# The delta rule's triangular inverse: four doublings on 32 by 32 diagonal blocks, held compactly

## The chip, the cores and the metric

The kernel runs on one core of a Trainium2 chip. The metric is the device time of one execution in microseconds (us). TensorE (PE) multiplies matrices, VectorE (DVE), ScalarE (ACT) and GpSimd (POOL) do elementwise work, SyncE (SP) issues transfers. Each engine works through its own list of instructions in order and waits at semaphores for the others.

## The reference, cut to what matters

The program is two layers of a network over 1024 positions of width 1024. The first layer mixes by a short convolution and sparse attention, the second by a gated delta rule with eight heads; each is followed by a gated feed-forward part and a gated embedding. The change lies in the delta rule of the second layer:

```python
kb = k * beta[..., None]
vb = v * beta[..., None]
m = jnp.where(strict, jnp.einsum('bhncd,bhnsd->bhncs', kb, k) * decay, 0.0)
t_inv = lax.linalg.triangular_solve(eye + m, jnp.broadcast_to(eye, m.shape), left_side=True, lower=True, unit_diagonal=True)
u = t_inv @ vb
w = t_inv @ (kb * jnp.exp(g)[..., None])

def step(state, xs):
    v_new = u_c - w_c @ state
    o = (q_c * jnp.exp(g_c)[..., None]) @ state + qk_c @ v_new
    state = state * jnp.exp(g_last)[..., None, None] + jnp.einsum('bhcd,bhce->bhde', k_dec, v_new)
```

For every head and chunk a unit triangular matrix is inverted; then a recurrence runs over the chunks of a head.

## The kernel before, in words

The delta rule is worked in chunks of 128 rows. A group is four chunks of one head, so eight heads of eight chunks make 16 groups. `l1_inv` (from line 1382) inverts the four matrices of a group side by side: `NM` holds minus the strict triangle, [128, 4, 128] in f32; `U` is to become the inverse (in transposed form) and `T` is its transpose.

The inverse grows by doublings. With the blocks of size n on the diagonal inverted, the off-diagonal block of size n in each pair follows from two products: `py` (NM times every second block of T's columns), copied out by ACT into `Y`, and `pz` (U times Y). DVE writes `pz` into the right places of `T` under a mask (`copy_predicated`, the masks are in `cm`), and a DVE transpose in 32 by 32 blocks gives `U` back. Lines 1460 to 1479 do this for n = 2, 4, 8 and 16 (k = 1 to 4) on full 128 by 128 matrices: four matmuls of 128x128 weights and 64 moving columns for `py`, four for `pz`. The first pairs (n = 1) come from POOL, lines 1457 and 1458: `NM` masked, plus the identity. The fifth doubling (lines 1482 to 1500, `py` with suffix 5) already works on 32 by 32 blocks, two or three positions of the array at once; the sixth (lines 1503 to 1514) on 64 by 64.

Each `yield` in `l1_inv` ends a step. `l1_mix` runs two groups' inverses alternately (two chains, ten steps apart), and between any two steps it lets a recurrence of an earlier group (`l1_rec`: `px`, `pn`, `pS`, `po`) take a step, and calls `F`, which issues some filling: matmuls of the projection (`l1_proj`, line 1340, 512 columns), after that of the output gate (`l1_z`, line 1589, 256 columns), near the end of the embedding (line 1022). How much filling stands between two steps follows from a count of steps and from fixed costs that each filling matmul yields, not from the steps' own length:

```python
us = max((L1_FILL - used[0]) / (2 * max(16 * L1_STEPS + L1_TAIL - done_steps, 1)), L1_MIN)
F(us)
rec()
F(us)
```

This is done under a manual schedule for TensorE, so TensorE executes the matmuls in just this order. The order of the other engines is chosen by a scheduler. `U` has three buffers, `T` and `Y` two.

Of the kernel before, what the change touches and what calls it, by code (L numbers as in the profile page):

```python
# [9 lines left out]
F32 = mybir.dt.float32  # L10
F32R = mybir.dt.float32r
BF16 = mybir.dt.bfloat16
I32 = mybir.dt.int32
U8 = mybir.dt.int8
AF = mybir.ActivationFunctionType
ALU = mybir.AluOpType
# [4 lines left out]
P = 128  # L21
# [14 lines left out]
QB0 = TOPK // P  # L36
NQB = NT - QB0

C_ID, C_CAUS, C_TRI, C_DM, C_UP0, C_ONE = 0, 128, 384, 512, 640, 768
NCF = 768  # L40


def _consts():
    r = np.arange(P)[:, None]
    c = np.arange(P)[None, :]
    f = np.zeros((P, NCF), np.float32)
    f[:, C_ID:C_ID + P] = r == c
    f[:, C_CAUS + P:C_CAUS + 2 * P] = np.where(c <= r, 0.0, NEG)
    f[:, C_TRI:C_TRI + P] = r <= c
    f[:, C_DM:C_DM + P] = np.where(c >= r, 0.0, NEG)  # L50
    f[:, C_UP0:C_UP0 + P] = (r // 2 == c // 2) & (r < c)
    m = np.zeros((P, 5, 64), np.int32)
    for k in range(1, 6):
        e = np.array([x for x in range(P) if not x >> k & 1])[None, :]
        m[:, k - 1] = ((((r ^ e) >> k) == 1) & (r > e))
    inv = lambda dim: (np.float32(1.0) / (np.float32(10000.0) ** (np.arange(0, dim, 2, dtype=np.float32) / np.float32(dim)))).astype(np.float32)
    fr = np.concatenate([inv(64), inv(32)])[None, :]
    return f, m, np.ascontiguousarray(fr)


class _K:
# [12 lines left out]
    def setup(self):  # L74
# [5 lines left out]
        self.dr = self.pool(self.es, "scr", space=DRAM)  # L80
        self.cf = self.const.tile([P, NCF], F32, name="cf")
        self.ident = self.cf[:, C_ID:C_ID + P]
# [1048 lines left out]
    def l1(self, close_h):  # L1131
        nc, A = self.nc, self.A
        self.oD = self.dr.tile([S, D], F32, name="oD")
        self.zD = self.dr.tile([S, D], F32, name="zD")
        self.cD = self.dr.tile([24, P, S], F32, name="cD")
        self.gD = self.dr.tile([2 * H, S], F32, name="gD")
        with self.phase("l1") as es:
            hp = self.pool(es, "l1hT")
            hT = self.hT_tiles((hp, hp), "1")
            sp = self.pool(es, "l1small")  # L1140
            self.cm = sp.tile([P, 5 * 64], I32, name="cm")
            nc.sync.dma_start(self.cm, A["cst_m"])
            da = self.pool(es, "l1a")
            cw = da.tile([P, 24, 4], F32, name="odcw")
            nc.sync.dma_start(cw, A["od_conv"])
            self.psum(es, "l1ps", tp0=1, tp1=1, st=2)
            self.ttags = itertools.cycle(["tp0", "tp1", "st", "st"])
            with ExitStack() as e2:
                nw = self.pool(e2, "l1norm")
                gB = self.bcast_row(self.np2, A["g_mix1"], D, "gB", "gB_mix1")  # L1150
                zab = self.l1_zab(nw, da, hT)
                for t in range(NT):
                    self.norm_T(self.np2, self.h[:, t, :], gB, hT, t, "n1", hnp=self.np)
                    if t:
                        next(zab)
                close_h()
                ab = [x for x in zab][-1]
                self.l1_gates(sp, nw, ab)
            db = self.pool(es, "l1b")
            self.goB = self.bcast_row(db, A["g_o"], P, "goB", "goB")  # L1160
            with self.tc.manual_schedule(engines={mybir.EngineType.PE}):
                self.l1_mix(da, db, hT, cw)
# [217 lines left out]
    def l1_inv(self, dp, hd, g, X, tag):  # L1380

        nc = self.nc
        v, gp = nc.vector, nc.gpsimd
        CH = lambda t: slice(t * P, (t + 1) * P)
        flat = lambda x: x.rearrange("p a b -> p (a b)")
        t0, nm = 4 * g, f"{hd}_{g}"
        X["step"] = 0
        G2 = lambda tg, bufs=2: dp.tile([P, 4, P], F32, tag=tg, bufs=bufs, name=f"{tg}{nm}")
# [52 lines left out]
        NM, AQ = G2("NM"), G2("AQ", 3)  # L1441
        X["step"] += 1
        yield True
        p = self.tp(f"pkk{nm}", tag)
# [6 lines left out]
        p = self.tp(f"pkq{nm}", tag)  # L1451
# [1 line left out]
            nc.tensor.matmul(p[:, CH(j)], kTn[:, j, :], cq[:, CH(j)], start=True, stop=True)  # L1453
        v.tensor_tensor(flat(AQ), p, flat(Dt), op=ALU.mult)

        U, T = G2("U", 3), G2("T")
        gp.tensor_tensor(U, NM, self.cf[:, None, C_UP0:C_UP0 + P].to_broadcast([P, 4, P]), op=ALU.mult)
        gp.tensor_tensor(U, U, self.ident[:, None, :].to_broadcast([P, 4, P]), op=ALU.add)
        v.transpose(flat(T), flat(U))
        for k in range(1, 5):  # L1460
            n = 2 ** k
            ev = lambda x: x.rearrange("p (b two n) -> p b two n", two=2, n=n)[:, :, 0, :]
            X["step"] += 1
            yield True
            py = self.tp(f"py{nm}_{k}", tag)
            for j in range(4):
                nc.tensor.matmul(py[:, j * 64:(j + 1) * 64], NM[:, j, :], ev(T[:, j, :]), start=True, stop=True)
            Y = G2("Y")
            nc.scalar.copy(flat(Y)[:, :256], py[:, :256])
            X["step"] += 1  # L1470
            yield True
            pz = self.tp(f"pz{nm}_{k}", tag)
            for j in range(4):
                nc.tensor.matmul(pz[:, j * 64:(j + 1) * 64], U[:, j, :], flat(Y)[:, j * 64:(j + 1) * 64], start=True, stop=True)
            sh = [P, 4, 64 // n, n]
            v.copy_predicated(T.rearrange("p a (b two n) -> p a b two n", two=2, n=n)[:, :, :, 0, :],
                              self.cm[:, (k - 1) * 64:k * 64].rearrange("p (b n) -> p b n", n=n)[:, None].to_broadcast(sh),
                              pz[:, :256].rearrange("p (a b n) -> p a b n", a=4, n=n))
            v.transpose(flat(U), flat(T))
        X["step"] += 1  # L1480
        yield True
        py = self.tp(f"py{nm}_5", tag)
        q = [slice(32 * x, 32 * x + 32) for x in range(4)]
        for j in range(4):
            for e, o in ((0, 1), (2, 3)):
                nc.tensor.matmul(py[q[o], q[j]], NM[q[e], j, q[o]], T[q[e], j, q[e]], start=True, stop=True)
        Y = G2("Y")
        for o in (1, 3):
            nc.scalar.copy(Y[q[o], 0, :], py[q[o], :P])
        X["step"] += 1  # L1490
        yield True
        pz = self.tp(f"pz{nm}_5", tag)
        for j in range(4):
            for e, o in ((0, 1), (2, 3)):
                nc.tensor.matmul(pz[q[e], q[j]], Y[q[o], 0, q[j]], U[q[o], j, q[o]], start=True, stop=True)
            nc.tensor.matmul(pz[q[1], q[j]], U[q[1], j, q[1]], Y[q[1], 0, q[j]], start=True, stop=True)
        blk = lambda x: pz[q[x], :P].rearrange("p (a b) -> p a b", a=4)
        v.tensor_copy(T[q[1], :, q[0]], blk(1))
        for e, o in ((0, 1), (2, 3)):
# [3 lines left out]
        py = self.tp(f"py6{nm}", tag)  # L1503
        for j in range(4):
            nc.tensor.matmul(py[64:, j * 64:(j + 1) * 64], NM[:64, j, 64:], T[:64, j, :64], start=True, stop=True)
        Y = G2("Y")
# [4 lines left out]
        pz = self.tp(f"pz6{nm}", tag)  # L1511
# [157 lines left out]

def _layout(I):  # L1670
    f, m, fr = _consts()
    L = {"cst_f": f, "cst_m": m.reshape(P, -1), "cst_fr": fr}
    I = {k: np.asarray(a) for k, a in I.items()}
# [48 lines left out]
```

## Time and profile before

| | us |
|---|---|
| median of three runs | 3055.42 (3049.29 to 3058.53) |
| the profiled execution | 3053.1 |
| its span, first to last instruction | 3051.3 |
| TensorE busy in the span | 2934.6 (96%) |
| DVE, ACT, POOL busy | 1911.4 (63%), 1269.5 (42%), 981.1 (32%) |
| projection matmuls (line 1340), first and last start | 1499.8 and 1988.7 |
| gate matmuls (line 1589), first and last start | 1989.0 and 2125.9 |
| first and last `py` of the four doublings (line 1467) | 1568.7 and 2112.0 |

How to read the rows: a timeline row gives start, duration, engine, line, what is written and from what, the tile of the array and the shapes; "x8" joins eight equal instructions in a row. An f32 matmul of the program shows as two records. Matmuls are pipelined, so records overlap, and a step's share of TensorE is seen from starts, not from durations. A row of lines has count, busy time, mean duration of one, and the idle time of the engine ahead of it.

### The profile page before, as it was taken

To read this page: it belongs to the slowest core of one execution; us is meant where nothing else is said; L and a number is where in the kernel's file an instruction comes from. 1 tells how busy PE (TensorE), PEld (TensorE's weight loads), DVE (VectorE), ACT (ScalarE), POOL (GpSimd) and SP (SyncE) were. 2 spreads that over 40 slices of the span, in tenths; PEclk is the share of its full clock that TensorE was granted. 3 is DMA by queue.
4 is the path that set the end of the run, shared out by engine and by line. 5 is a ranking of instruction groups with operands and counts; after the bars stand their busy time and mean duration, and the time that the engine had idled before them with its cause. 6 is when DMAs were issued, how large, how long until landed. Compare 5 with 4: busy or idle time off the path is not lost. (4 is left out here: it accounts for less than half of the span.)

```text
span 3051.3 us, 41382 instructions
## 1 busy us (share of the span) xinstructions
PE 2934.6 (96%) x16139; PEld 2473.5 (81%) x16139; DVE 1911.4 (63%) x3274; ACT 1269.5 (42%) x2225; POOL 981.1 (32%) x755
## 2 busy tenths in 40 slices
PE   7999999999999999999999999999999999989999
PEld 7989877787888877778888888898677888877877
DVE  5799985555444458963567777764545444458861
ACT  3558725544333334342445554443223333334341
POOL 1341000124444446523122222221134444455342
PEclk9999998999999999999999999999999999999999
DMA  4113174201222226423242222222721222254422
GB/s 143 49 49 100 47 242 152 90 28 73 104 104 104 101 101 257 135 100 120 85 144 96 81 91 90 91 87 89 274 76 66 104 104 104 104 198 164 137 92 90
DMA packets 119796, 340.55 MB, mean 112 GB/s; under 512 B 11568, under 2 KB 34608, under 8 KB 101936
## 3 DMA queue, kind: packets, MB, share of 16 engines
q1 hardware_dynamic: 119600, 337.91, 31.7%
q8 instruction: 127, 2.08, 0.3%
q14 instruction: 69, 0.57, 0.1%
HBM read 240.81 MB, written 97.06 MB: 111 GB/s over the span
## 5 line engine op out<-in xcount | busy, mean ns | idle before, releaser
L992 PE MATMUL pda<-sl 128*128 128x512 f32 x1056 | 251.4, 397 | 17.6 <-ACT sl L981 7.3
L992 PEld LDWEIGHTS pda<-sl 128*128 128x128 f32 x1056 | 202.3, 192 | 63.4 <-ACT sl L981 8.1
L778 POOL TENSOR_TENSOR S<-wr_gu 128x512 f32<-128x512 f32 x44 | 67.6, 1536 | 398.8 <-DMA wr_gu<-in_w_gu_dram 349.9
L992 PE MATMUL pdb<-sl 128*128 128x512 f32 x792 | 185.4, 392 | 2.1 <-ACT sl L981 1.1
L106 DVE TENSOR_TENSOR w2l_gu<-S,w2h_gu 128x1024 fp32r<-128x1024 f32 x44 | 73.4, 1667 | 173.9 <-ACT w2h_gu L105 173.9
L992 PEld LDWEIGHTS pdb<-sl 128*128 128x128 f32 x792 | 149.4, 189 | 34.6 <-DVE sl L982 1.9
L1340 PE MATMUL pso<-hh,wl_od 128*128 128x512 f32 x384 | 161.4, 420 | 0.0
L1340 PE MATMUL pso<-hl,wh_od 128*128 128x512 f32 x384 | 161.3, 420 | 0.0
L1340 PE MATMUL pso<-hh,wh_od 128*128 128x512 f32 x384 | 161.0, 419 | 0.0
L982 DVE TENSOR_TENSOR sl<-sl 128x1536 fp32r<-128x1536 f32 (+1 forms) x56 | 110.9, 1989 | 37.1 <-ACT sl L981 37.1
L981 ACT CAST sl<-sl 128x1536 fp32r<-128x1536 f32 (+1 forms) x56 | 76.6, 1374 | 133.2 <-DMA sl<-gfD 133.2
L1358 DVE SCALAR_TENSOR_TENSOR c<-pso,odcw,c 128x509 f32<-128x509 f32 (+1 forms) x144 | 107.1, 744 | 19.4 <-ACT c L1355 17.5
L776 POOL TENSOR_TENSOR T_dn<-wr_dn 128x512 f32<-128x512 f32 x44 | 78.9, 1821 | 101.1 <-PE pgb L847 52.1
L224 PE MATMUL pskqv<-wh_kqv,hh 128*128 128x256 f32 x384 | 109.5, 286 | 0.3 <-ACT wh_kqv L105 0.3
L224 PE MATMUL pskqv<-wh_kqv,hl 128*128 128x256 f32 x384 | 108.7, 283 | 0.0
L224 PE MATMUL pskqv<-wl_kqv,hh 128*128 128x256 f32 x384 | 108.3, 283 | 0.0
L105 ACT CAST w2h_gu<-S 128x1024 fp32r<-128x1024 f32 x44 | 46.3, 1052 | 147.1 <-PE pga L847 147.1
L600 DVE TENSOR_SCALAR_CACHE_REDUCE tk_junk<-sc,tk_f 128x1024 int8<-128x1024 f32 (+5 forms) x111 | 102.6, 924 | 1.8
L1110 PE MATMUL psp<-wh_pg,hh_p 128*128 128x512 f32 x256 | 101.6, 397 | 0.0
L1110 PE MATMUL psp<-wl_pg,hh_p 128*128 128x512 f32 x256 | 100.6, 393 | 0.0
L1110 PE MATMUL psp<-wh_pg,hl_p 128*128 128x512 f32 x256 | 100.5, 393 | 0.0
L597 ACT ACTIVATE tk_junka<-sc,tk_f 128x512 int8<-128x512 f32 (+2 forms) x93 | 83.7, 900 | 36.8 <-DVE tk_f L615 30.5
(531 smaller groups left out, 9055.6 us busy)
## 6 DMA issues: line engine op xcount, KB each, us to landing
wr_gu<-in_w_gu_dram SPq DMA_DIRECT2D x44, 1024.0 KB
sl<-gfD SPq DMA_DIRECT2D x42, 768.0 KB
gfD<-Sg SPq DMA_DIRECT2D x22, 1024.0 KB
wr_dn<-in_w_dn_dram SPq DMA_DIRECT2D x22, 1024.0 KB
wr_od<-in_w_qkv_dram SPq DMA_DIRECT2D x12, 1024.0 KB
cD<-c SPq DMA_DIRECT2D x24, 512.0 KB
gfD<-g SPq DMA_DIRECT2D x22, 512.0 KB
wr_z<-in_w_z_dram SPq DMA_DIRECT2D x10, 1024.0 KB
```

The source lines that it names most:

```text
L106: self.nc.vector.tensor_tensor(lo, src, hi.bitcast(F32), op=ALU.subtract).ins)
L224: nc.tensor.matmul(out, a[:, kc, c], b[:, kc, :], start=(kc == 0 and i == 0), stop=(kc == KC - 1 and i == 2))
L597: nc.scalar.activation(jk[:, :n], sc[b], AF.Sign, bias=fb, scale=-1.0, accum_out=c)
L600: v.tensor_scalar(jk[:, :n], sc[b], fb, 0.0, op0=op, op1=ALU.add, accum_out=c)
L776: sub = lambda o, x, y: eng.tensor_tensor(o, x, y, op=ALU.subtract)
L778: eng.tensor_tensor(dst[0], b[2], b[3], op=ALU.add)
L981: nc.scalar.copy(y, x.bitcast(F32))
L982: v.tensor_tensor(x, x.bitcast(F32), y.bitcast(F32), op=ALU.subtract)
L992: nc.tensor.matmul(ps, a[:, i, c], b[:, i, :], start=first and i == 0 and k == 0, stop=i == m - 1 and k == 2, skip_group_check=True)
L1110: nc.tensor.matmul(ps, a[:, kc, c], b, start=kc == 0 and i == 0, stop=kc == KC - 1 and i == 2)
L1340: nc.tensor.matmul(ps[:, f * 512:(f + 1) * 512], a[:, kc, :], b[f][:, kc, :], start=(kc == 0 and i == 0), stop=(kc == KC - 1 and i == 2))
L1358: nc.vector.scalar_tensor_tensor(c[:, e:(f + 1) * 512], ps[:, e - d:(f + 1) * 512 - d], cw[:, k:k + 1], c[:, e:(f + 1) * 512], op0=ALU.mul ...
```

## The change

The first four doublings touch only the 32 by 32 blocks on the diagonal. The changed kernel holds these blocks compactly: `U32` and `T32` are [128, 4, 32] tiles in which the 32 rows of block b lie on partitions 32b to 32b+31. A `py` or `pz` step is now 16 matmuls (four chunks, four blocks), each with 32x32 weights and 16 moving columns, on the four diagonal positions of the array. The ACT copy, the predicated copy and the DVE transpose work on the compact tiles, a quarter as long. `U` and `T` are filled with zeros by POOL at the start, and after the fourth doubling POOL copies the blocks into them (four copies for `U`, two for `T`, which is only kept as its upper left 64 rows and columns). The first pairs are four POOL products on 32 partitions and one sum. The fifth doubling reads `U32` and `T32`. The masks shrink to four of 16 columns, and the constants change to suit.

```diff
-        U, T = G2("U", 3), G2("T")
-        gp.tensor_tensor(U, NM, self.cf[:, None, C_UP0:C_UP0 + P].to_broadcast([P, 4, P]), op=ALU.mult)
-        gp.tensor_tensor(U, U, self.ident[:, None, :].to_broadcast([P, 4, P]), op=ALU.add)
-        v.transpose(flat(T), flat(U))
+        q = B32
+        small = lambda tg, n=32: dp.tile([P, 4, n], F32, tag=tg, bufs=2, name=f"{tg}{nm}")
+        U, T = G2("U", 3), small("T", 64)
+        gp.memset(U, 0.0)
+        gp.memset(T[:64], 0.0)
+        U32, T32 = small("U32"), small("T32")
+        for b in q:
+            gp.tensor_tensor(U32[b], NM[b, :, b], self.cf[b, None, C_UP0:C_UP0 + 32].to_broadcast([32, 4, 32]), op=ALU.mult)
+        gp.tensor_tensor(U32, U32, self.cf[:, None, C_I32:C_I32 + 32].to_broadcast([P, 4, 32]), op=ALU.add)
+        v.transpose(flat(T32), flat(U32))
...
             for j in range(4):
-                nc.tensor.matmul(py[:, j * 64:(j + 1) * 64], NM[:, j, :], ev(T[:, j, :]), start=True, stop=True)
-            Y = G2("Y")
-            nc.scalar.copy(flat(Y)[:, :256], py[:, :256])
+                for b in q:
+                    nc.tensor.matmul(py[b, j * 16:(j + 1) * 16], NM[b, j, b], ev(T32[b, j, :]), start=True, stop=True)
+            Y = small("Yc", 16)
+            nc.scalar.copy(flat(Y), py[:, :64])
...
             for j in range(4):
-                nc.tensor.matmul(pz[:, j * 64:(j + 1) * 64], U[:, j, :], flat(Y)[:, j * 64:(j + 1) * 64], start=True, stop=True)
-            sh = [P, 4, 64 // n, n]
-            v.copy_predicated(T.rearrange("p a (b two n) -> p a b two n", two=2, n=n)[:, :, :, 0, :],
-                              self.cm[:, (k - 1) * 64:k * 64].rearrange("p (b n) -> p b n", n=n)[:, None].to_broadcast(sh),
-                              pz[:, :256].rearrange("p (a b n) -> p a b n", a=4, n=n))
-            v.transpose(flat(U), flat(T))
+                for b in q:
+                    nc.tensor.matmul(pz[b, j * 16:(j + 1) * 16], U32[b, j, :], Y[b, j, :], start=True, stop=True)
+            sh = [P, 4, 16 // n, n]
+            v.copy_predicated(T32.rearrange("p a (b two n) -> p a b two n", two=2, n=n)[:, :, :, 0, :],
+                              self.cm[:, (k - 1) * 16:k * 16].rearrange("p (b n) -> p b n", n=n)[:, None].to_broadcast(sh),
+                              pz[:, :64].rearrange("p (a b n) -> p a b n", a=4, n=n))
+            v.transpose(flat(U32), flat(T32))
+        for b in q:
+            gp.tensor_scalar(U[b, :, b], U32[b], 1.0, None, op0=ALU.mult)
+        for b in q[:2]:
+            gp.tensor_scalar(T[b, :, b], T32[b], 1.0, None, op0=ALU.mult)
...
-                nc.tensor.matmul(py[q[o], q[j]], NM[q[e], j, q[o]], T[q[e], j, q[e]], start=True, stop=True)
+                nc.tensor.matmul(py[q[o], q[j]], NM[q[e], j, q[o]], T32[q[e], j, :], start=True, stop=True)
...
-                nc.tensor.matmul(pz[q[e], q[j]], Y[q[o], 0, q[j]], U[q[o], j, q[o]], start=True, stop=True)
-            nc.tensor.matmul(pz[q[1], q[j]], U[q[1], j, q[1]], Y[q[1], 0, q[j]], start=True, stop=True)
+                nc.tensor.matmul(pz[q[e], q[j]], Y[q[o], 0, q[j]], U32[q[o], j, :], start=True, stop=True)
+            nc.tensor.matmul(pz[q[1], q[j]], U32[q[1], j, :], Y[q[1], 0, q[j]], start=True, stop=True)
```

TensorE, where a group's second chain ends its fourth doubling and the next group begins its first (names: `pso` is the filling, `pz_1_4` the fourth `pz` of one group, `py_0_1` the first `py` of the next). Before:

```order
L1340 MATMUL pso_13949<-hl_1_11707,wh_od_13176 128x512
L1340 MATMUL pso_13949<-hh_1_11706,wl_od_13177 128x512
L1474 MATMUL pz_1_4_14114<-Y_1_14078,U_1_13754 128x64 x4
L1340 MATMUL pso_13949<-hh_1_11706,wh_od_13176 128x512
L1340 MATMUL pso_13949<-hl_1_11707,wh_od_13176 128x512
L1340 MATMUL pso_13949<-hh_1_11706,wl_od_13177 128x512
L1340 MATMUL pso_13949<-hh_1_11706,wh_od_13176 128x512
L1467 MATMUL py_0_1_14143<-T_0_14095,NM_0_14022 128x64 x4
L1340 MATMUL pso_13949<-hl_1_11707,wh_od_13176 128x512
```

The same place in the changed kernel:

```order
L1343 MATMUL pso_14319<-hl_1_11707,wh_od_13340 128x512
L1343 MATMUL pso_14319<-hh_1_11706,wl_od_13341 128x512
L1485 MATMUL pz_1_4_14539<-Yc_1_14496,U_1_14085 32x16 x16
L1343 MATMUL pso_14319<-hh_1_11706,wh_od_13340 128x512
L1343 MATMUL pso_14319<-hl_1_11707,wh_od_13340 128x512
L1343 MATMUL pso_14319<-hh_1_11706,wl_od_13341 128x512
L1343 MATMUL pso_14319<-hh_1_11706,wh_od_13340 128x512
L1477 MATMUL py_0_1_14586<-T_0_14517,NM_0_14416 32x16 x16
L1343 MATMUL pso_14319<-hl_1_11707,wh_od_13340 128x512
```

Nothing has moved: each step of four matmuls has become one of sixteen small ones at the same place, with the same filling around it.

POOL, at the start of the same group's inverse (`kd` belongs to the group, `qe`, `dec` and `egl` to later ones; brackets name the semaphores waited for; `U32` and `T32` are printed as U and T). Before:

```order
L1439 TENSOR_TENSOR kd_0_14020<-kR_0_13856,dec_0_13837 128x512 [waits DVE_49,Activation_49]
L1457 TENSOR_TENSOR U_0_14094<-NM_0_14022,cf 128x512 [waits DVE_49]
L1458 TENSOR_TENSOR U_0_14094<-U_0_14094,cf 128x512 [waits Pool_49]
L1398 TENSOR_TENSOR qe_1_14276<-lq_1_13891,EGb_1_13897 128x512 [waits DMAHW4_49,DMAHW1_49,PE_49]
L1400 TENSOR_SCALAR egl_1_14278<-EGb_1_13897 128x4 [waits DVE_49]
```

In the changed kernel:

```order
L1442 TENSOR_TENSOR kd_0_14414<-kR_0_14214,dec_0_14195 128x512 [waits DVE_49,Activation_49]
L1466 TENSOR_TENSOR U_0_14516<-NM_0_14416,cf 32x128 [waits DVE_49]
L1466 TENSOR_TENSOR U_0_14516<-NM_0_14416,cf 32x128 [waits Pool_49]
L1466 TENSOR_TENSOR U_0_14516<-NM_0_14416,cf 32x128 x2
L1462 MEMSET U_1_15085 128x512 [waits PE_49,Pool_49]
L1467 TENSOR_TENSOR U_0_14516<-U_0_14516,cf 128x128
L1401 TENSOR_TENSOR qe_1_14779<-lq_1_14261,EGb_1_14267 128x512 [waits DMAHW4_49,DMAHW1_49,PE_49]
L1403 TENSOR_SCALAR egl_1_14781<-EGb_1_14267 128x4 [waits DVE_49]
L1494 TENSOR_SCALAR T_1_14082<-T_1_14086 32x4x32 [waits DVE_49]
L1494 TENSOR_SCALAR T_1_14082<-T_1_14086 32x4x32 [waits Pool_49]
```

Two operations have become five, the zeros for the next group's `U` stand between the products and the sum, and the copies into `T` come after `qe`. The memset's semaphore of PE is that of the last `pn` which reads the buffer's former `U`, in the recurrence three groups back; on TensorE that `pn` stands ahead of this group's `pkq` (line 1453), which stands ahead of the `pz_1_4` above.

## Rows read from the trace of the kernel before

**Rows 1.** Windows in the stage: us, busy us and instructions per engine, clock, DMA, GB/s.

```profile
core 0: us, PE busy (x) PEld busy (x) DVE busy (x) ACT busy (x) POOL busy (x), PEclk, DMA share, GB/s
1700.00:1850.00 150.00, 148.38 (x1124) 126.84 (x1123) 110.83 (x323) 76.39 (x177) 41.90 (x43) 1.00 0.27 92
1989.00:2126.00 137.00, 136.27 (x1325) 132.07 (x1324) 74.87 (x240) 49.42 (x128) 25.59 (x24) 1.00 0.22 76
```

**Rows 2.** Waits of TensorE, 1560 to 2126 us: total us, times, longest.

```profile
PE pS L1546 <- DVE vn L1542: 2.6, 4, 1.2
PE pz L1495 <- ACT Y L1489: 2.3, 2, 1.7
```

**Rows 3.** Lines, 1560 to 2126 us, TensorE: count, busy us, mean ns, idle before.

```profile
L1467 PE MATMUL py<-T,NM 128*128 128x64 f32 x512 | 64.8, 270 | 0.1
```

**Rows 4.** Line 1467 alone, 1988.9 to 2126 us: ns min/median/max, first and last start.

```profile
L1467 PE MATMUL py<-T,NM x120: 217/275/275, 1990.9 to 2112.0; 128*128 128x64 f32 x120
```

**Rows 5.** Timeline of TensorE between 512-column matmuls: start us, us, instruction.

```profile
1704.49 0.39 PE L1340 MATMUL pso<-hh,wh_od 128*128 128x512 f32 x1
1704.71 1.00 PE L1467 MATMUL py<-T,NM 128*128 128x64 f32 x8
...
1705.84 0.39 PE L1340 MATMUL pso<-hh,wl_od 128*128 128x512 f32 x1
...
1706.29 0.40 PE L1340 MATMUL pso<-hl,wh_od 128*128 128x512 f32 x1
1706.62 0.44 PE L1486 MATMUL py<-T,NM 32*32 32x32 f32 x16
...
1707.32 0.40 PE L1340 MATMUL pso<-hh,wh_od 128*128 128x512 f32 x1
...
1709.61 0.40 PE L1340 MATMUL pso<-hh,wh_od 128*128 128x512 f32 x1
1709.93 0.22 PE L1495 MATMUL pz<-U,Y 32*32 32x32 f32 x2
...
1710.19 0.19 PE L1496 MATMUL pz<-Y,U 32*32 32x32 f32 x1
...
1710.65 0.40 PE L1340 MATMUL pso<-hh,wl_od 128*128 128x512 f32 x1
```

**Rows 6.** Timeline of TensorE between 256-column matmuls.

```profile
2074.14 0.28 PE L1589 MATMUL psz<-wl_z,hh 128*128 128x256 f32 x1
2074.26 1.00 PE L1467 MATMUL py<-T,NM 128*128 128x64 f32 x8
...
2075.28 0.28 PE L1589 MATMUL psz<-wh_z,hh 128*128 128x256 f32 x1
...
2081.70 0.28 PE L1589 MATMUL psz<-wl_z,hh 128*128 128x256 f32 x1
2081.91 0.44 PE L1486 MATMUL py<-T,NM 32*32 32x32 f32 x16
...
2082.51 0.28 PE L1589 MATMUL psz<-wh_z,hh 128*128 128x256 f32 x1
```

**Rows 7.** Timeline at the start of one inverse; brackets: idle before, releaser.

```profile
1697.42 1.13 DVE L1448 SCALAR_TENSOR_TENSOR NM<-pkk,nbeta,Dt 128x128 f32<-128x128 f32 x4 [1.12 <-PE pkk L1446]
...
1698.62 1.28 POOL L1457 TENSOR_TENSOR U<-NM,cf 128x512 f32<-128x512 f32 x1 [9.97 <-DVE NM L1448]
...
1699.72 0.38 PE L1540 MATMUL pn<-x,U 128*128 128x128 f32 x2
...
1699.98 1.28 POOL L1458 TENSOR_TENSOR U<-U,cf 128x512 f32<-128x512 f32 x1
...
1701.29 0.71 DVE L1459 STREAM_TRANSPOSE T<-U 128x512 f32<-128x512 f32 x1 [0.80 <-POOL U L1458]
```

**Rows 8.** Lines, 1560 to 2126 us, small operations of DVE and POOL.

```profile
L1542 DVE TENSOR_SCALAR vn<-pn,beta 128x128 f32<-128x128 f32 x60 | 20.5, 342 | 19.4 <-PE pn L1540 19.1
...
L1392 POOL TENSOR_TENSOR dec<-Dt,G 128x4 f32<-128x4 f32 x14 | 2.9, 206 | 24.4 <-DMA Dt<-gD 21.0 <-DVE rsq_a L135 1.6 <-DVE rsq_y L137 1.4
```

More of the change, by code (lines that the diff above doesn't have):

```diff
@@ L37 @@
 NQB = NT - QB0
-C_ID, C_CAUS, C_TRI, C_DM, C_UP0, C_ONE = 0, 128, 384, 512, 640, 768
-NCF = 768
+C_ID, C_CAUS, C_TRI, C_DM, C_UP0, C_I32 = 0, 128, 384, 512, 640, 672
+NCF = 704
+B32 = [slice(32 * x, 32 * x + 32) for x in range(4)]
 def _consts():
@@ L50, in _consts @@
     f[:, C_DM:C_DM + P] = np.where(c >= r, 0.0, NEG)
[L51 to L54, printed above, removed]
+    r, c = r % 32, c[:, :32]
+    f[:, C_UP0:C_UP0 + 32] = (r // 2 == c // 2) & (r < c)
+    f[:, C_I32:C_I32 + 32] = r == c
+    m = np.zeros((P, 4, 16), np.int32)
+    for k in range(1, 5):
+        e = np.array([x for x in range(32) if not x >> k & 1])[None, :]
         m[:, k - 1] = ((((r ^ e) >> k) == 1) & (r > e))
@@ L1140, in l1 @@
             sp = self.pool(es, "l1small")
-            self.cm = sp.tile([P, 5 * 64], I32, name="cm")
+            self.cm = sp.tile([P, 4 * 16], I32, name="cm")
             nc.sync.dma_start(self.cm, A["cst_m"])
@@ L1482, in l1_inv @@
         py = self.tp(f"py{nm}_5", tag)
-        q = [slice(32 * x, 32 * x + 32) for x in range(4)]
         for j in range(4):
             for e, o in ((0, 1), (2, 3)):
-                nc.tensor.matmul(py[q[o], q[j]], NM[q[e], j, q[o]], T[q[e], j, q[e]], start=True, stop=True)
+                nc.tensor.matmul(py[q[o], q[j]], NM[q[e], j, q[o]], T32[q[e], j, :], start=True, stop=True)
         Y = G2("Y")
```

## Prediction

> **What bounds the kernel now.** I read the windows first, cut at the borders of the delta-net stage (the second mixer: `l1_mix`, from the first inverse step at about 1560 us to the last gate matmul at 2126 us). In 1700 to 1850 TensorE is busy 148.38 of 150 us and in 1989 to 2126 it is busy 136.27 of 137, while DVE, ACT and POOL have 110.83, 76.39 and 41.90 of 150 us in the first of these [rows 1]. The reader is to see that this stage ends when TensorE has worked through its list, and that the list never runs dry: the work of the inverse stands between matmuls of the projection (L1340) and later of the gate (L1589), which need nothing from it. The waits of TensorE in the stage come second: the two longest entries are 2.6 and 2.3 us in total, so almost nothing is lost to late operands [rows 2]. A gain must therefore be a shorter TensorE list, and a shorter latency alone would bring nothing.
>
> How long an instruction stands in that list is not its duration, since matmuls overlap. It is read from starts in the timeline: from the last filling matmul ahead of a step to the second one behind it, because the first one behind also starts late.
>
> **The step that is changed.** Per group of four 128-row chunks the four doublings take a `py` and a `pz` each; with 16 groups that is 128 steps. The lines show it: 512 records of `py`, eight a step (four f32 matmuls, each recorded twice), so 64 steps [rows 3]; `pz` has the same loop. 120 of these 512 fall after 1988.9 us, where the filling is the gate's 256 columns wide [rows 4]: 15 `py`, with as many `pz` 30 steps; the other 98 stand between 512-column matmuls.
>
> - Cost now. Between 512-column matmuls: 1704.49 to 1705.84, 1.35 us for a step and two fillings [rows 5]. Between 256-column ones: 2074.14 to 2075.28, 1.14 us [rows 6].
> - Cost then. A step becomes 16 matmuls (32 records) of 32x32 weights and 16 moving columns, four blocks on the diagonal, each with rows and columns of the array to itself. No row shows four such blocks at once, but the fifth doubling is the same thing with fewer: `py_5` has 16 records on two blocks and takes 1706.29 to 1707.32, 1.03 us; `pz_5` has 24 records on three blocks and takes 1709.61 to 1710.65, 1.04 us [rows 5]. Eight records more cost 0.01 us: the 24 starts lie between 1709.93 and 1710.19, 0.26 us, and the 16 of `py_5` take as long (0.44 less one record's 0.19). So the time goes by rounds (four chunks, two records each, eight rounds of about 0.031 us), and another block in a round is nearly free. I take 0.01 more for the fourth block, 1.05 us. Between 256-column matmuls `py_5` takes 2081.70 to 2082.51, 0.81 us [rows 6]; two more blocks make 0.83. Both spans hold the idle time ahead of small blocks, which these steps already pay.
> - Bounds. Below: if a round follows the moving columns, of which there are 16 instead of 32, half of the 0.25 us goes, 0.125 us a step or 16 us in all on top. Above: if the four blocks took a round each, 32 times 0.031 us is 1.00 instead of 0.25 us, the step 1.79 us, slower than now. I stay with 1.05, next to the nearest row.
> - Sum. 98 x (1.35 - 1.05) + 30 x (1.14 - 0.83) = 29.4 + 9.3 = 38.7 us off TensorE's list.
>
> Here a rule speaks against the change. In the rows above two row groups of `py_5` write into one `py` tile of 512 f32 a partition, and their starts don't line up behind each other. The Trainium skill (TensorEngine Tiling (Array Packing), Gotcha 1: PSUM Pressure) says that different row tiles cannot access the same PSUM bank at once. By it the four blocks, all in one tile, would go one after another and the sum would be that of the upper bound; the trace does not agree for two row groups, so I give it a small chance for four. A second page (TensorE: Matmul & The Clock Gate, the section "Wait — 56ns, not 53.3ns?") has a floor of about 25 ns from start to start: 32 of these are an estimated 0.8 us, which would also undo the gain; 24 starts in 0.26 us (11 ns each) don't agree with it for different blocks.
>
> **What else it moves.** TensorE's order in the stage stays as it was, step for step, so each step keeps the filling around it.
>
> - Evacuation and transposes shrink: 80 DVE transposes of 128x512 at 0.71 us become 128x128, 64 predicated copies go from 256 to 64 elements a partition, 64 ACT copies too. These engines aren't the bound, so I cost it at nothing; it shortens every latency between steps, by as much as the filling between them shortens.
> - The start of the inverse: POOL made `U` by two operations of 1.28 us after DVE's last `NM` (end 1698.55), DVE's transpose ended at 1702.00, and the first `py` began at 1704.71: 2.7 us in hand [rows 5, 7]. Now POOL does four small products, for every other group a memset of the next group's `U`, and one sum. Bounds for a small one (128 elements a partition): 0.206 us, the row with 4, and 1.28, the row with 512 [rows 7, 8]; by elements between them 0.47 us, which I take. The memset at most 1.28. With 0.08 us between operations (the gap of the two POOL rows) 5 x 0.47 + 1.28 + 6 x 0.08 = 4.1 us, then at most 0.71 for the transpose: 1703.4. The memset waits for a `pn` of the recurrence that began at 1699.72 and took 0.38 us here [rows 7], earlier than the products end (about 1700.8), so this wait is free; behind it stand the sum and, through the transpose, `py`. One shortened `pz` lies between, so `py` would start at 1704.4: 1 us still in hand.
> - The six copies back into `U` and `T`: two of `T` (1.1 us) are needed by the sixth doubling, behind `py_5` and `pz_5`, which alone stand 3.3 us apart (1706.62 and 1709.93) [rows 5]; `U`'s later still. Hidden. In all POOL loses 32 x 1.28 = 41 us and gets at most 16 x (11 x 0.47 + 1.28 + 0.64) = 114, the second memset taken at half the first. Its busy share of a quarter has the room.
>
> I add 1 us for new waits: 3053.1 (the profiled execution, 3051.3 of span and 1.8 around it) - 38.7 + 1 = 3015.4. The median shown is 2.3 above the profiled execution, so 3017.7, say 3018.
>
> **Rivals.**
>
> 1. The recurrence takes part of it back. Between `px`, `pn` and `pS` DVE must answer (`vn` has 60 instructions [rows 8], `x` about as many), and about half of these 120 answers have a shortened step beside them. If each lost the whole 0.30 us, 60 x 0.30 = 18 us come back: 3036. For it: the longest wait on the list is just this one, `pS` for `vn` [rows 2]. Against: 2.6 us over 60 is next to nothing, so most have slack, and DVE is relieved.
> 2. Only two blocks run at once. 16 rounds are 0.50 us, the step 1.30: 128 x 0.05 = 6 us off, 3049, no change that can be measured. For it: two blocks with both rows and columns of their own are all that a row shows (the third of `pz_5` shares its rows with another). Against: that third one was free though it shares. The same time comes out if every small POOL operation cost 1.28 us: the chain then takes 6 x 1.28 + 0.5 + 0.7 = 8.9 us after 1698.6 and ends 3.1 us after 1704.4; over 16 groups with the memset in half of them, some 40 us of waits cancel the gain. The 0.206 us row speaks against it.
> 3. Slower: the four blocks take a round each, because they share a PSUM tile or cannot start in so quick a sequence. Place: the 128 steps; price: 1.79 - 1.35 = 0.44 us each, 56 us, so 3111. It turns to a loss when 32 starts take more than 0.25 + 0.30 = 0.55 us, 17 ns a start. Against: 11 ns a start with three blocks [rows 5].
>
> **How the numbers follow.** Forecast 0.76 (3006 to 3026, by the bounds of the step's cost), first rival 0.10 (3026 to 3040), second 0.08, third 0.06. A difference below 0.3% (9 us) cannot be told from none: faster 0.86, same 0.08, slower 0.06. The range from 3006 to 3038 holds the forecast and most of the first rival.
>
> **What would show it.** In the profile after: the `py` and `pz` steps between 512-column matmuls at 1.0 to 1.1 us from the filling ahead to the second behind, with 32 starts inside 0.3 us; the stage from the first projection matmul to the last gate matmul shorter by 36 to 40 us; TensorE's waits in the stage still below 8 us, none of `py` on POOL's `U`; everything behind the stage as long as before. Wrong it is if four blocks stretch the starts, if `py` waits for the transpose at the beginning of a group, or if the granted clock, 1.00 in both windows [rows 1] (the 2.4 GHz level), falls in the stage because the steps hold more idle time in relation to work.

## The result, and the profile after

| | before | changed | |
|---|---|---|---|
| median of runs | 3052.36 us (4 runs, 3043.74 to 3058.53) | 3018.2 us (4 runs, 3012.98 to 3021.66) | ratio 0.9889, 95% interval 0.9859 to 0.9919 |
| measured again, another chip | 3054.2 us (7 runs) | 3012.37 us (4 runs, 3010.24 to 3017.35) | ratio 0.9868, 0.9849 to 0.9886 |
| profiled execution | 3053.1 us | 3017.34 us | -35.8 us |

The kernel became 34 to 42 us (1.1 to 1.3%) faster; 3018 had been forecast.

The first reading is of windows. Two of the changed kernel lie inside the two fillings, as those of [rows 1] did (same columns):

```profile
1700.00:1850.00 150.00, 147.22 (x2100) 112.01 (x2097) 106.14 (x340) 81.10 (x189) 59.33 (x90) 1.00 0.32 104
1960.00:2091.00 131.00, 128.39 (x2086) 118.53 (x2083) 67.33 (x240) 48.73 (x133) 44.99 (x69) 1.00 0.26 82
```

TensorE is still busy for 98% of both, so its list still sets the end of the stage. The bound has not moved to another engine; the list has become shorter. By how much is read from the first projection matmul to the last gate matmul. The two groups of matmuls by their lines, before (ns min/median/max, first and last start):

```profile
L1340 PE MATMUL pso<-hh,wh_od x384: 387/395/628, 1499.8 to 1987.4; 128*128 128x512 f32 x192
...
L1589 PE MATMUL psz<-wh_z,hl x192: 274/283/385, 1989.2 to 2125.9; 128*128 128x256 f32 x192
```

and after:

```profile
L1343 PE MATMUL pso<-hh,wh_od x384: 387/396/628, 1504.8 to 1960.8; 128*128 128x512 f32 x192
...
L1603 PE MATMUL psz<-wh_z,hl x192: 276/282/387, 1962.3 to 2091.0; 128*128 128x256 f32 x192
```

The window over this stretch, before:

```profile
1499.80:2126.00 626.20, 620.18 (x4741) 544.09 (x4740) 423.00 (x1228) 288.50 (x652) 140.10 (x142) 1.00 0.27 91
```

and after:

```profile
1504.70:2091.20 586.50, 577.70 (x7814) 467.66 (x7813) 378.96 (x1228) 278.58 (x652) 202.06 (x313) 1.00 0.30 98
```

The stage lasts 586.2 us (1504.8 to 2091.0) instead of 626.1, 39.9 less, though TensorE has 3073 records more in it. DVE has 44 us less to do there, ACT 10 us less, POOL 62 more. Behind the stage nothing changed: the program ends 924.6 us after the last gate matmul, 925.4 before. The stage began 5.0 us later than in the profile of before, which is why the span is only 35.7 us shorter.

Where the 39.9 us come from, the step shows. The timeline of TensorE between 512-column matmuls, to be laid beside the first rows of [rows 5]:

```profile
1699.25 0.40 PE L1343 MATMUL pso<-hh,wh_od 128*128 128x512 f32 x1
1699.58 0.44 PE L1477 MATMUL py<-T,NM 32*32 32x16 f32 x32
1699.95 0.50 PE L1343 MATMUL pso<-hl,wh_od 128*128 128x512 f32 x1
1700.29 0.39 PE L1343 MATMUL pso<-hh,wl_od 128*128 128x512 f32 x1
...
2042.89 0.28 PE L1603 MATMUL psz<-wl_z,hh 128*128 128x256 f32 x1
2043.10 0.44 PE L1477 MATMUL py<-T,NM 32*32 32x16 f32 x32
2043.47 0.38 PE L1603 MATMUL psz<-wh_z,hl 128*128 128x256 f32 x1
2043.69 0.28 PE L1603 MATMUL psz<-wh_z,hh 128*128 128x256 f32 x1
```

From the filling ahead to the second one behind it are 1.04 us, and 0.80 in the 256-column part, answering to [rows 6]. The first block matmul starts 0.33 us behind the filling; 32 of them start in 0.26 us (0.44 less one record's 0.18); 0.11 us later comes the filling, and 0.34 after it the next. Two fillings alone take 0.46 us (1698.79 to 1699.25 in the same timeline). So a step is 0.26 us of starts and 0.31 us that TensorE needs to go over to the small blocks and back. The medians over all steps between two such fillings without a wait are 1.032 and 0.802 us; measured in the same way before they are 1.355 and 1.131. The list became shorter by 98 x 0.323 + 30 x 0.329 = 41.5 us.

What came back are waits. TensorE's waits in the stage, 1560 to 2091 us (total us, times, longest), answering to [rows 2]:

```profile
PE tpk L1439 <- DVE kR L1415: 1.9, 2, 0.9
PE pz L1485 <- ACT Yc L1479: 1.6, 1, 1.6
PE pS L1560 <- DVE vn L1556: 1.5, 3, 1.0
PE py L1519 <- POOL o L1580: 1.0, 1, 1.0
```

With six smaller entries (2.3 us in all) they come to 8.3 us, against 5.9 before (two smaller entries included). The gaps of TensorE over the whole stage, the width of the two windows above less its busy time, are 8.8 us, against 6.0.

The last of these rows names POOL, but it is no wait for POOL's new copies. The `py` of the sixth doubling waits for DVE, ACT and POOL at once; POOL's copies into `T` had ended at 1959.16, and the `py` came right behind ACT's copy into `U`:

```profile
1965.97 0.51 ACT L1514 COPY U<-pz 32x128 f32<-32x128 f32 x2
...
1966.57 0.65 PE L1519 MATMUL py<-T,NM 64*64 64x64 f32 x8 [0.98 <-POOL o L1580]
```

The start of an inverse, answering to [rows 7] (brackets: idle before, releaser):

```profile
1692.84 1.13 DVE L1451 SCALAR_TENSOR_TENSOR NM<-pkk,nbeta,Dt 128x128 f32<-128x128 f32 x4 [1.45 <-PE pkk L1449]
...
1694.04 1.97 POOL L1466 TENSOR_TENSOR U<-NM,cf 32x128 f32<-32x128 f32 x4 [7.24 <-DVE NM L1451]
...
1696.08 0.53 POOL L1462 MEMSET U<- 128x512 f32 x1
1696.66 0.46 POOL L1467 TENSOR_TENSOR U<-U,cf 128x128 f32<-128x128 f32 x1
1697.20 0.30 DVE L1468 STREAM_TRANSPOSE T<-U 128x128 f32<-128x128 f32 x1
```

`T32` is there at 1697.50, 3.5 us after the last `NM`, just as long as before (1698.55 to 1702.00); the `py` that reads it starts at 1699.58, so 2.1 us are in hand.

### The profile page after: what moved, and what is told of

It reads as the page before. It is cut to its first block, busy times and chain, and to the rows that moved or that the text cites. A ratio compares the mean times of both kernels' runs of the same rounds, so it can differ in the third digit from the quotient of the medians.

```text
span 3015.6 us, 47722 instructions
## 1 busy us (share of the span) xinstructions
PE 2891.6 (96%) x19211; PEld 2396.3 (79%) x19211; DVE 1873.3 (62%) x3274; ACT 1259.5 (42%) x2225; POOL 1043.9 (35%) x931
```

## The experiments

All are edits of the changed kernel, timed against the kernel before on the same chip. "Stage" is the time from the first projection matmul to the last gate matmul, 586.2 and 585.0 us in two profiles of the changed kernel. Where the granted clock fell, "lost to the clock" is an estimate, the sum over windows of 2 us of width times (1 - clock): 1.7 and 0.0 us in these two profiles, 1.7 in that of before. The theory was that the gain is the shorter step on TensorE's list and nothing else; the rivals put it on shorter evacuations and transposes, or saw a cost on POOL that eats part of it.

**1. The long transposes back.** `U32` and `T32` lie in tiles four times as wide, so the transpose is 128x512 again; the matmuls stay.

```diff
-        U32, T32 = small("U32"), small("T32")
+        Uw, Tw = small("U32", 128), small("T32", 128)
+        gp.memset(Uw, 0.0)
+        gp.memset(Tw, 0.0)
+        U32, T32 = Uw[:, :, :32], Tw[:, :, :32]
...
-            v.transpose(flat(U32), flat(T32))
+            v.transpose(flat(Uw), flat(Tw))
```

> The changed kernel, but U32 and T32 lie in tiles four times as wide and DVE transposes all 128x512 again (80 transposes at about 0.71 us instead of 0.31, some 32 us more work for DVE, and 0.4 us more between a step and the one two steps on); POOL fills the wide tiles with zeros. TensorE's list is that of the changed kernel. My theory (the gain is TensorE's shorter list alone): as the changed kernel, within 3 us of 3018, steps still 1.03 us apart. Rival (part of the gain is the relief of DVE and the shorter latency): 10 to 20 us of the gain are lost, about 3030 to 3040, with TensorE's waits on DVE grown by as much.

Measured: 3015.8 us, ratio 0.9878 (0.9862 to 0.9893), stage 587.4. The line of the transpose in the changed kernel (count, busy us, mean ns, idle before):

```profile
L1490 DVE STREAM_TRANSPOSE U<-T 128x128 f32<-128x128 f32 x64 | 19.8, 309 | 0.8
```

and in this one:

```profile
L1493 DVE STREAM_TRANSPOSE U<-T 128x512 f32<-128x512 f32 x64 | 45.3, 708 | 0.8
```

Each step's answer from DVE takes 0.40 us longer and the time is that of the changed kernel. TensorE's gaps are 11.4 us, 2.3 to 2.6 more than in the two profiles of the changed kernel (8.8 and 9.1), so the shorter transposes are worth some 2 us at most. The copies of ACT and DVE stayed short here; the next experiment covers them.

**2. Block by block.** The same 16 matmuls in another order: all four chunks of one block, then the next block.

```diff
-            for j in range(4):
-                for b in q:
+            for b in q:
+                for j in range(4):
```

> The changed kernel with the two loops of a step exchanged: all four chunks of one block, then the next block, so that eight records in a row fall on the same position of the array. Same matmuls, same data. My theory (records of one position follow each other at 0.031 us, records of different positions run side by side): a step's 32 starts take about 32 x 0.031 = 1.0 us instead of 0.25, the step 1.78 us instead of 1.03, and the kernel 128 x 0.75 = 96 us longer than the changed one, about 3114, slower than before. Rival (starts are paced by something that counts records, such as the issue of instructions): no change, 3018. In between, if the queue can look past the records of one position: 0.3 to 0.6 us a step, 3030 to 3060.

Measured: 3068.8 us, ratio 1.0054 (1.0039 to 1.0069), stage 639.7. Slower than before, by the order of 16 matmuls. The step (TensorE, start and duration):

```profile
1701.48 0.40 PE L1343 MATMUL pso<-hh,wh_od 128*128 128x512 f32 x1
1701.81 0.88 PE L1477 MATMUL py<-T,NM 32*32 32x16 f32 x32
1702.62 0.50 PE L1343 MATMUL pso<-hl,wh_od 128*128 128x512 f32 x1
1702.95 0.39 PE L1343 MATMUL pso<-hh,wl_od 128*128 128x512 f32 x1
```

1.47 us instead of 1.04; 32 starts take 0.70 us instead of 0.26. The single records show why. Four records of each step last 198 ns, the others about 178; read as the first record of each block, these four start at 0, 153, 307 and 460 ns. From its first one a block's eight records follow each other after 52 ns and then after 31 to 32, so the next block begins when five of the eight have started. In the changed kernel's order the four long records start at 0, 7, 13 and 20 ns, and each block then goes on at the same distances. So the blocks run wholly beside each other only if they come in turn; block by block they overlap by less than half. Everything else of the change, the shorter copies and transposes too, is still in this kernel, and the whole gain is gone: the gain lies in the matmuls. By the medians of the step (1.472 and 1.242) the stage should be 98 x 0.117 + 30 x 0.111 = 14.8 us longer than before; it is 13.6 longer (with 5.1 us lost to the clock, 3.4 more than before). The expected 3114 was too high, since it left out the overlap at each change of block. The point at which the gain was to turn to a loss, 0.55 us for 32 starts, lies between the two measured values.

**3. Twice the moving columns.** Full 32 columns of `T32` and `Yc` instead of every second block.

```diff
-                    nc.tensor.matmul(py[b, j * 16:(j + 1) * 16], NM[b, j, b], ev(T32[b, j, :]), start=True, stop=True)
-            Y = small("Yc", 16)
+                    nc.tensor.matmul(py[b, j * 32:(j + 1) * 32], NM[b, j, b], T32[b, j, :], start=True, stop=True)
+            Y = small("Yc", 32)
```

> The changed kernel with all 32 moving columns in each block matmul instead of the 16 that are needed (ACT then copies 128 columns instead of 64, about 0.05 us more each). My theory (a round is set by the loading of the 32-column weights, not by the moving columns): starts still within 0.26 us, step 1.03, kernel within 3 us of 3018. Rival (a round follows the moving columns, or four blocks of 32 columns crowd the PSUM tile): the starts take 0.35 to 0.5 us and the kernel is 12 to 32 us longer, 3030 to 3050.

Measured: 3012.21 us, ratio 0.9868 (0.9852 to 0.9884), stage 588.7. The step's record:

```profile
1702.34 0.45 PE L1477 MATMUL py<-T,NM 32*32 32x32 f32 x32
```

Its starts take 0.45 less 0.19, 0.26 us, as with 16 columns. Here a round of four blocks does not follow the moving columns; the lower bound of the forecast (a round that follows them) is out. By the median the step is 1.045 us, 0.013 longer, and the kernel is 6 us below the forecast, no more than two measurements of the changed kernel differ (experiment 10).

**4. Every block matmul twice.**

```diff
-            for j in range(4):
+            for j in (0, 1, 2, 3, 0, 1, 2, 3):
```

> The changed kernel with every block matmul of the four doublings issued twice (64 records a step, same result). My theory (TensorE's list ends the stage, each round of four blocks costs 0.031 us): 0.25 us more a step, 128 x 0.25 = 32 us, 3050, about as long as before. Rival (the steps lie in time that TensorE would spend waiting anyway): under 10 us more, below 3028.

Measured: 3070.96 us, ratio 1.0057 (1.0035 to 1.0079), stage 639.5, 53 us longer than the changed kernel's. Two steps in TensorE's timeline, the second behind a wait (in brackets):

```profile
1700.52 0.73 PE L1477 MATMUL py<-T,NM 32*32 32x16 f32 x64
...
1927.36 1.03 PE L1485 MATMUL pz<-Yc,U 32*32 32x16 f32 x64 [2.75 <-ACT Yc L1479]
```

The list of TensorE's waits has these together (total us, times, longest):

```profile
PE pz L1485 <- ACT Yc L1479: 8.8, 6, 2.7
```

And the windows from the end of two of them on, the one of 2.75 us and one of 1.28 (columns as in [rows 1]):

```profile
1926.00:1942.00 16.00, 14.64 (x252) 10.33 (x252) 5.46 (x11) 6.42 (x15) 5.53 (x9) 0.57 0.14 52
2002.00:2018.00 16.00, 15.79 (x276) 14.16 (x277) 9.17 (x16) 5.10 (x13) 4.87 (x7) 0.57 0.27 85
```

The step itself does what eight more rounds should: 64 starts take 0.55 us (0.73 less 0.18), and it grows by 0.287 us by the medians, 36.7 us over 128. TensorE's gaps grow by 2.8 us (8.8 to 11.6). The rest is the clock: the two windows show a granted clock of 0.57, mostly the 1.2 GHz level, and 17.0 us are lost so over the stage, 15.3 more than in the changed kernel. Together that is 54.8 for the 53.3 measured. The expectation had the first term alone and missed by 21 us. The experiment says both that a step's price is its rounds, and that stretches at the lower clock behind a few waits can cost more than the waits last.

**5. POOL's copies twice.**

```diff
-        for b in q:
+        for b in q + q:
             gp.tensor_scalar(U[b, :, b], U32[b], 1.0, None, op0=ALU.mult)
-        for b in q[:2]:
+        for b in q[:2] + q[:2]:
```

> The changed kernel with POOL's six copies of the blocks into U and T issued twice in each group (16 x 6 x 0.55 us, some 53 us more work for POOL). My theory (POOL's new work is hidden behind the steps between the fourth and the sixth doubling): as the changed kernel, within 4 us of 3018. Rival (TensorE's waits for T and U in the sixth doubling come from these copies): 1 to 3 us more in each group, 3035 to 3065, with waits of the py of the sixth doubling on POOL.

Measured: 3014.46 us, ratio 0.9875 (0.9852 to 0.9899), stage 584.3. TensorE's only wait for these copies is this one:

```profile
PE pz L1527 <- POOL U L1492: 1.1, 3, 0.6
```

Some 53 us more on POOL (the two lines have 35.0 and 18.2 us in the changed kernel) cost 1.1 us of waits. The copies back are hidden, with room for as many again.

**6. Half the blocks.** Only blocks 0 and 1 are multiplied; the work on blocks 2 and 3 in the four doublings is left out.

```diff
-                for b in q:
+                for b in q[:2]:
```

> The changed kernel with only the first two of the four blocks multiplied in the four doublings (16 records a step instead of 32; the products of the blocks of rows 64 to 127 are left out, and the copies of their results). My theory (a step lasts eight rounds, however many different blocks are in each): a step still 1.03 us, kernel within 3 us of 3018. Rival (the starts are counted one by one, 8 ns each): 0.13 us less a step, 16 us off, 3002.

Measured: 3021.14 us, ratio 0.9899 (0.9876 to 0.9923), stage 591.1. A step in TensorE's timeline:

```profile
1702.27 0.43 PE L1477 MATMUL py<-T,NM 32*32 32x16 f32 x16
```

16 starts take 0.25 us, 32 took 0.26. Over the step's medians (1.018 and 0.789) half the matmuls save 98 x 0.014 + 30 x 0.013 = 1.8 us; the profile loses more than that to waits (3.2 us more of gaps) and to the clock (6.8 us, 5.1 more), and the kernel is 3 us above the forecast instead of 16 below. So blocks three and four are nearly free, 0.014 us for both, as the forecast had worked out from two and three.

**7 and 8. Two steps back to back.** If 0.31 us of a step are the way to the small blocks and back, two small steps without filling between them should pay it once. The planner was changed to issue the steps of the two chains back to back while both are in their doublings, with the chains 5 (first) or 3 steps apart instead of 10 and four buffers instead of three for what a group holds: 40 and 56 pairs.

```diff
-... L1_SKEW, ... = ... 10, ...
+... L1_SKEW, ... = ... 5, ...
...
+            both = all(x is not None and 6 <= data[x[0]]["step"] <= 15 for x in chains)
...
+                if both:
+                    if c:
+                        F(us / 2)
+                        rec()
+                        F(3 * us)
+                        rec()
+                        F(us / 2)
+                    continue
```

> A version meant to be faster: the chains stand five steps apart instead of ten, with four buffers instead of three for what the recurrence reads, and where both chains are at a step of small blocks (doublings one to five) these two steps stand back to back without filling between them (40 such pairs), the filling being put around them and between two steps of the recurrence. If the 0.31 us that a step costs beside its starts is idle time at the change from full matmuls to blocks and back, each pair saves it once: 40 x 0.31 = 12 us off the changed kernel, less about 5 us for a recurrence that ends later, 3011. Rival (the 0.31 us belongs to each step): no gain, 3018 to 3025. A second rival: answers of DVE and ACT come too close together in the pairs and TensorE waits, above 3025.

> The same with the chains three steps apart: some 56 pairs. If the idle time is shared, 56 x 0.31 = 17 us less, with about 11 us for the recurrence's later end: 3012. Rivals as for five steps apart.

Measured: 3054.04 us, ratio 1.0003 (0.9988 to 1.0019), stage 612.7 at five steps; 3035.24 us, ratio 0.9939 (0.992 to 0.9959), stage 603.1 at three. Both missed. The pair does what it should; the timeline of TensorE, three steps apart:

```profile
1717.37 0.40 PE L1352 MATMUL pso<-hh,wl_od 128*128 128x512 f32 x1
1717.70 0.44 PE L1494 MATMUL pz<-Yc,U 32*32 32x16 f32 x32
1717.97 0.45 PE L1486 MATMUL py<-T,NM 32*32 32x16 f32 x32
1718.35 0.50 PE L1352 MATMUL pso<-hh,wh_od 128*128 128x512 f32 x1
```

and the longest entries in its list of TensorE's waits:

```profile
PE pS L1569 <- DVE vn L1565: 8.3, 7, 2.3
PE pn L1563 <- ACT oj L1581: 8.3, 4, 4.6
PE pn L1563 <- DVE x L1560: 4.2, 5, 2.3
PE px L1558 <- DVE S L1574: 4.1, 4, 1.7
```

The second step's records follow the first's after 0.27 us, and the slot with both takes 1.315 us by the median, where two slots of the changed kernel have 2 x (1.032 - 0.46) = 1.14 us beside their filling and this one 0.86: 0.29 us saved a pair, 16 us over 56. But the gaps of TensorE rose from 8.8 to 32.2 us (35.3 at five steps), and 8.5 us went to the clock (6.8 at five). Behind the stage the program takes 6.7 us longer than the changed kernel (11.4 at five steps), for the later end of the recurrence 11 and 5 had been allowed. Most of the waits stand in the recurrence. That it and the two chains now reach DVE and ACT together would explain them, but isn't shown.

**9. The same pairs with the chains as they were**, ten steps apart and with three buffers; 14 pairs are left.

> The changed kernel with its chains still ten steps apart and three buffers, and only those 14 pairs of steps put back to back that meet at this distance. A pair saves about 0.29 us of idle time (1.32 us for two steps and two fillings instead of 2 x 1.03 less two fillings of 0.46), so 14 x 0.29 = 4 us: 3014, no more than can just be told. Rival (the rearranged filling makes TensorE wait, as with five and three steps): 3020 to 3030 and gaps of more than 15 us in the stage. This tells whether the loss with five and three steps came from pairing or from the shorter distance of the chains.

Measured: 3015.36 us, ratio 0.9885 (0.9865 to 0.9905), stage 583.1, gaps 11.0. The stage is 2 to 3 us shorter than the changed kernel's, with nothing lost to the clock; the time cannot be told from it (3018.2 and 3012.37). So 14 such pairs do no harm. The loss of 7 and 8 came with what these two have beside them: the shorter distance of the chains, more pairs, a fourth buffer. No run parts these three, and that pairing gains in the end isn't shown either.

**10. The changed kernel once more**, beside the ninth.

> The changed kernel itself once more, beside the kernel before on the same chip, for a narrower ratio and a second profile. My theory: ratio 0.988 (0.986 to 0.990), stage 586 us from the first projection matmul to the last gate matmul; the first projection matmul between 1499 and 1505 us after the start whatever the kernel, so that the 4.9 us by which it came later in the first profile are no effect of the change. Rival: it starts at about 1504.8 again, by something that the change does ahead of the stage.

Measured: 3012.37 us, ratio 0.9868 (0.9849 to 0.9886), stage 585.0, gaps 9.1. The first projection matmul starts at 1506.8 us, outside the expected 1499 to 1505 and nearer to the rival; what that means stands in the next section under "Not foreseen". The run also sets how far two measurements of one kernel lie apart: 6 us. None of the variants beats the changed kernel by more than that.

## Why the prediction was right, point by point

- **What bounds.** Right. TensorE's list set the stage's end before and sets it now; experiment 1 (0.40 us longer transposes, no loss) and 5 (POOL's copies twice, 1.1 us) show that the other engines' work has room.
- **The step.** Forecast 1.05 and 0.83 us, measured 1.032 and 0.802. The reading by rounds was right: eight rounds, however many blocks stand in them, as long as they come in turn. Two, three (forecast), four blocks take 0.25 to 0.26 us of starts (experiment 6, [rows 5], the changed kernel), and 16 or 32 columns make no difference (experiment 3). The 0.01 us added for a fourth block is of the right size: two blocks more cost 0.014 (experiment 6).
- **The sum.** 41.5 us instead of 38.7. The step at 1.032 instead of 1.05 makes 98 x 0.018 = 1.8 us of the difference, the one at 0.802 instead of 0.83 another 0.8; the cost before was read rightly (medians 1.355 and 1.131).
- **New waits.** Mis-sized: 2.8 us of gaps more (2.4 by the list of waits), forecast 1. The list of waits was to stay below 8 us and came to 8.3. None of them is a `py` waiting for POOL's `U`. 41.5 less 2.8 is 38.7; the stage lost 39.9, and 1.2 us are not itemised.
- **POOL.** Right in the whole, off in the parts: small products 450 ns and the sum 457 (forecast 470), copies 547 and 570 on the mean, the memset 529, for which 1.28 us had been allowed. So the chain from `NM` to `T32` is as long as before instead of 1.4 us longer. POOL's busy time in the stage rose by 62 us (forecast up to 114 - 41 = 73). The lines, 1560 to 2100 us:

```profile
L1492 POOL TENSOR_SCALAR U<-U 32x128 f32<-32x128 f32 x64 | 35.0, 547 | 3.9
L1466 POOL TENSOR_TENSOR U<-NM,cf 32x128 f32<-32x128 f32 x64 | 28.8, 450 | 73.8 <-DVE NM L1451 71.0
...
L1467 POOL TENSOR_TENSOR U<-U,cf 128x128 f32<-128x128 f32 x16 | 7.3, 457 | 0.7
L1462 POOL MEMSET U<- 128x512 f32 x13 | 6.9, 529 | 5.3 <-DVE AQ L1457 3.2 <-PE pn L1554 1.6
```

- **First rival** (18 us come back in the recurrence): did not happen. `pS` waits for `vn` for 1.5 us in all, 2.6 before. Experiment 8 shows that the mechanism exists: there DVE's answers in the recurrence (`vn`, `x` and `S`) hold TensorE up for 16.6 us.
- **Second rival** (two blocks at once): out. Two blocks in a round would be 0.50 us for 32 starts; they take 0.26.
- **Third rival** (one block after another): not in this order of the loops, but it was closer than its chance of 0.06 says. Experiment 2 is its mechanism, 0.70 us of starts and a time above that of before. What decides is that the four blocks come in turn, and the forecast did not weigh the order.
- **The two rules.** By the Trainium skill (TensorEngine Tiling (Array Packing), Gotcha 1: PSUM Pressure) row tiles can't use one PSUM bank at once. Four of them write into one tile here and start 6 to 12 ns apart, so the traces do not agree for this shape. The Trainium skill (TensorE: Matmul & The Clock Gate, the section "Wait — 56ns, not 53.3ns?") has a floor of about 25 ns from start to start. The records of one block keep to it (31 to 32 ns in experiment 2), those of different blocks do not (5 to 12 ns). The Trainium skill (TensorEngine Tiling (Array Packing), section Key Properties) also says that a change of tiling mode drains TensorE. With that agree the 0.31 us of every step and the 0.29 us that a pair saves, though no row shows a drain as such.
- **Not foreseen.** The stage starts 5.0 us later in the profile after. The windows ahead of it, before and after, hold the same work of TensorE, so the 5.0 us are waits:

```profile
0.00:1499.80 1499.80, 1428.86 (x7518) 1214.92 (x7519) 980.17 (x1503) 665.38 (x1103) 465.78 (x340) 0.97 0.32 110
0.00:1504.80 1504.80, 1428.84 (x7519) 1213.16 (x7520) 979.50 (x1503) 665.08 (x1103) 464.14 (x345) 0.98 0.32 110
```

  Over the eleven profiles of the changed kernel and its variants, all with the same 7518 records of TensorE ahead of the stage, it starts between 1499.1 (three steps apart) and 1506.8 us. Of before there is one profile, 1499.8. So the change need not have caused it; whether it did stays open. The profiled execution was forecast at 3015.4 and took 3017.3: 5.0 us from the later start, less 2.2 in the stage (588.4 forecast, 586.2) and 0.8 behind it. The second measurement of the median, 3012.37, is 5.6 us below the forecast. So the closeness of the first median is partly luck. That of the stage is less so: 2.8 us too little for the steps and 1.8 too little for the waits stand against each other in it.

## What to carry to other kernels

Where TensorE's list is the bound, price a small step by starts, from the filling ahead to the second filling behind, and split it into rounds and the fixed price of going to small blocks and back. Blocks on different positions of the array are nearly free beside each other when they are issued in turn; issued one position at a time the same matmuls can cost more than the full-size ones. On a list that is full to 98%, moving the chains nearer to each other and pairing their steps saved 16 us of steps and lost more than that in waits.

## What the runs showed of the hardware that was not expected

- Two records on one 32x32 position start 31 to 32 ns apart (52 for the first two of a step), two on different positions 5 to 12 where the blocks come in turn; a round of four f32 blocks takes 32 ns with 16 moving columns as with 32.
- Between 128x128 matmuls a stretch of 32x32 ones costs 0.31 us once, however many they are (16, 32 or 64 records).
- A single wait of TensorE can be followed by a stretch at 1.2 GHz. The timeline of the changed kernel has:

```profile
1582.56 0.44 PE L1485 MATMUL pz<-Yc,U 32*32 32x16 f32 x32 [1.55 <-ACT Yc L1479]
...
1583.27 0.39 PE L1343 MATMUL pso<-hl,wh_od 128*128 128x512 f32 x1
1583.50 0.59 PE L1343 MATMUL pso<-hh,wl_od 128*128 128x512 f32 x1
```

and the window behind it:

```profile
1583.50:1586.90 3.40, 3.40 (x40) 2.32 (x39) 2.61 (x6) 0.69 (x2) 0.00 (x0) 0.51 0.91 294
```

The engine had waited 1.55 us ahead of the `pz`; the granted clock of the window is 0.51, so an estimated 1.7 us are lost in it, and wait and lower clock together cost twice the wait's length. In experiment 4 waits of 2.75 and of 1.28 us were each followed by a much longer stretch (the windows from 1926 and from 2002 us), while in the ninth experiment the list of waits has one of 2.3 us and the clock did not fall at all. What decides it the runs don't show.
